# An encoder layer with two kinds of attention: when TensorE multiplies the attention weights with the values

## The chip, the cores and the metric

The kernel runs on one core of one Trainium2 chip. A core has five engines that run side by side and wait for each other through semaphores: TensorE (PE in the profile; its weight loads are shown apart as PEld), VectorE (DVE), ScalarE (ACT), GpSimd (POOL) and SyncE (SP), whose queue issues nearly all transfers here. Each engine works through its own instructions in the program's order. The metric is the device time of one execution in microseconds, and less is better. A time is given as the median of several runs.

## The reference, cut to what matters

The reference is one inference step of an encoder layer. Two streams are computed: a prompt of 2048 frames (new) and 8 running streams with 16 frames each and a cache of 512. What the change touches is the prompt's attention, which exists in two kinds. Per head and per tile of 128 queries:

```python
# branch a: differential attention, 4 heads, block-causal
s = einsum('bqhcd,bkhcd->bhcqk', q, k) * HEAD_DIM_A ** -0.5
p = softmax(where(mask, s, -inf))
w = p[:, :, 0] - lam * p[:, :, 1]
o = einsum('bhqk,bkhe->bqhe', w, v)
# branch b: stick-breaking attention, 8 heads, causal
z = einsum('bqhd,bkhd->bhqk', q, k) * HEAD_DIM_B ** -0.5
log_1m = where(mask, log_sigmoid(-z), 0)
log_a = log_sigmoid(z) + reverse_cumsum(log_1m) - log_1m
a = where(mask, exp(log_a), 0)
o = einsum('bhqk,bkhd->bqhd', a, v)
```

Around it stand a modulated norm, one wide input projection (queries, keys, values and gates of both branches), and behind it the merge of the branches, an output projection and a last norm.

## The kernel before, in words

All matrix products are made in float16 pairs: a number is split into a high and a low half, and two or three products are added up. The program has three stages. The first (to about 150 us of the profile) makes the modulation and the normed input. The second, the main loop (to about 1845 us), makes the projections and the prompt's attention. The third makes the merge, the output and the attention of the running streams.

**The main loop** runs over 8 units of 17 steps each. Even units are heads of the softmax kind (`kind` 0), odd units are pairs of heads of the stick kind (`kind` 1). In a unit the step `NT` (16) stands for the running streams' tile and has no attention in this loop; the steps 0 to 15 are the prompt's tiles of 128 queries. Tile t meets t + 1 blocks of 128 keys, so a step's work grows with t.

**One tile's attention** takes this way. TensorE multiplies queries with keys in chunks of up to 512 keys (`chunk`, L656, L657, and the mask with L660) into one of three score banks `ps_s`. VectorE (softmax kind, L575) or ScalarE and VectorE (stick kind, L123 and the scan L633) empty the bank into `sc_p` and `sc_n`. The weights follow: `softmax_pair` for the softmax kind, `stick_weights` (a product on POOL, L639) for the stick kind. `turn` splits them into halves (`sc_n` again) and lets SP issue a transposing transfer into a tile `wt` (L597). These tiles are a ring of 5 (`WT_BUFS`), and one holds a segment of up to 8 key blocks (`SEG`); a softmax tile has one segment up to t = 7 and two from t = 8, a stick tile twice as many, for its two heads. At last TensorE multiplies the transposed weights with the values, block by block (`pv_block`): three products of 128 columns for the softmax kind (L713 to L715), one of 128 and one of 64 for the stick kind (L717, L718), added up in one of two banks `ps_o`. `natural` and `store` then take the result out.

**What sets the order.** The program is written step by step, and in a step three streams are laid into each other by `interleave`: `pieces` of the projections of later tiles (two products of 512 columns each, L445 and L521), the score chunks `qk` of this step's tile, and the products with values `vs` of the tile two steps earlier (`PV_LAG = 2`). Each piece has a weight, and a stream's pieces are spread evenly over the step by their weights; the products with values are spread over the stretch from 0.1 to 1.0 of it. A scheduler then orders each engine's instructions once, when the program is built: it may draw an instruction ahead of another that it takes to be not ready yet. In the running program that order is fixed, so a product with values whose `wt` has not landed holds all that stands behind it on TensorE.

SP's queue is shared by the transposing transfers, the loads of projected inputs (`hs`, L422), the stores of results (`out_dram`, `o_d`, `z_d`, `g_d`) and the caches' loads.

Of the kernel before, what the change touches and what calls it, by code (L numbers as in the profile page):

```python
# [32 lines left out]
NT = SEQ // P  # L33
# [3 lines left out]
NEG = -3.0e38  # L37
STICK = 14
SEG = 8
PV_LAG = 2  # L40
WT_BUFS = 5
SC_BUFS = 6
V_LO, V_HI = 0.1, 1.0
W_READY = 9
WIDE_BUFS = 6
P0_AT = 2.0, 4.0, 6.0
# [45 lines left out]
    return c  # L92


def interleave(*streams):

    order = []
    for i, pieces in enumerate(streams):  # L100
        lo, hi = 0.0, 1.0
        if isinstance(pieces, tuple):
            pieces, lo, hi = pieces
        total = sum(cost for cost, _ in pieces) or 1.0
        done = 0.0
        for j, (cost, fn) in enumerate(pieces):
            order.append((lo + (hi - lo) * (done + cost / 2) / total, i, j, fn))
            done += cost
    for _, _, _, fn in sorted(order, key=lambda e: e[:3]):
        fn()  # L110


# [1 line left out]
def layer_kernel(ctx: ExitStack, tc: tile.TileContext, a: dict):  # L114
# [81 lines left out]
    def bank(tag, dt=F32):  # L196
        return ps.tile([P, 512 if dt == F32 else 1024], dt, tag=tag, name=f"ps_{tag}", bufs=BANKS[tag])
# [384 lines left out]
    def turn(job, seg, scale=None):  # L582

        nb = seg["hi"] - seg["lo"]
        nk = nb * P
        w16 = seg["n"].bitcast(F16)
        hi, lo, src = w16[:, 0:nk], w16[:, nk : 2 * nk], seg["p"][:, 0:nk]
        if scale is None:
            S.copy(out=hi, in_=src)  # L589
            V.tensor_tensor(out=lo, in0=src, in1=hi, op=ALU.subtract)  # L590
        else:
            split(hi, lo, src, scale, S)
        if job["t"] == NT:
            seg["wt"] = job["pool"].tile([P, 10, P], F16, tag="dwt", name="dwt", bufs=2)
        else:
            seg["wt"] = wtp.tile([P, 2 * SEG, P], F16, tag="wt", name="wt", bufs=WT_BUFS)
        nc.sync.dma_start_transpose(out=seg["wt"][:, 0 : 2 * nb, :], in_=w16[:, 0 : 2 * nk])  # L597

    def softmax_pair(job):

# [102 lines left out]
    def store(U, t, o):  # L703
        ui = (U["h"] + 4 * U["kind"]) * P
        if U["kind"] == 0:
            sum_squares(o, P, osums[:, t, U["h"] : U["h"] + 1])
        load(out=o_d[t][:, ui : ui + P], in_=o)
# [9 lines left out]
            T.matmul(po[:, c * P : (c + 1) * P], wt[:, wj, :], vt[:, c, :, :], start=first, stop=False)  # L717
            T.matmul(po[:, c * P : c * P + 64], wt[:, nb + wj, :], vt[:, c, 0, :], start=False, stop=last)  # L718

    def pv(job):  # L720

        U, t, c = job["U"], job["t"], job["c"]
        segs = job["segs"] if U["kind"] == 0 else job["segs"][::-1]
        order = [(seg, j) for seg in segs for j in range(seg["hi"] - seg["lo"])]

        def block(i):
            seg, j = order[i]
            if i == 0 and (U["kind"] == 0 or c == 0):
                U["po", t] = bank("o")
            pv_block(job, seg, U["po", t], j, U["v"][seg["lo"] + j], i == 0, i == len(order) - 1)  # L730
            if i == len(order) - 1 and (U["kind"] == 0 or c == 1):
                store(U, t, natural(U, t, U.pop(("po", t))))

        return [(1.5, lambda i=i: block(i)) for i in range(len(order))]

    def cache_column(name, h):
        return "ab".index(name[0]) * 4 + h
# [167 lines left out]
    steps = [(u, t) for u in range(8) for t in [NT] + list(range(NT))]  # L905
    back = []
    spare, cached = norms()
    jobs = []


    line = []
# [58 lines left out]
    with tc.tile_pool(name="p0", bufs=1) as p0:  # L970
# [28 lines left out]
        first = wide_tile().rearrange("p k n -> p (k n)")  # L999
# [207 lines left out]
    cuts = None  # L1207
# [98 lines left out]

        return [branch_weight for _ in branch_weights] + [rest] + [lambda t=t: first(t) for t in tiles[0:2]]

    for n in range(len(steps) + PV_LAG):
        made, qk, vs = [], [], []  # L1310
        if n < len(steps):
            u, t = steps[n]
            past += duration(t)
            if t == (3 if u == 0 else NT) and u < 7:
                back += prepare_unit(u + 1)
            if u == 7 and not back and not spare and not cached and len(branch_weights) > 1:
                branch_weight()
            for fn in back[: -(-len(back) // max(1, (W_READY if u else W_READY + 2) - t % NT))]:
                back.pop(0)()
            for todo, here in ((spare, norm_at), (cached, keys_at)):  # L1320
                if todo and here(u, t):
                    left = sum(here(*step) for step in steps[n:])
                    for _ in todo[: -(-len(todo) // left)]:
                        todo.pop(0)()
            if t < NT:
                qk = scores(units[u], t, made)
        if n >= PV_LAG:
            for job in jobs[n - PV_LAG]:
                vs += pv(job)
        target = position(len(steps) * past / whole + LEAD)  # L1330
        pieces = take(target, min(n + 1, len(steps) - 1))
        if at[0] == len(line) and not pieces and not spare and not cached:
            if cuts is None:
                cuts = early_work()
            pieces = [(1.0, fn) for fn in cuts[: -(-len(cuts) // (len(steps) + PV_LAG - n))]]
            del cuts[: len(pieces)]
        interleave(pieces, qk, (vs, V_LO, V_HI))
        jobs.append(made)
    c01.close()


    with ExitStack() as c2:
# [7 lines left out]
        vs = scales(total(add_up_all(csums), 8), res, "s_c", 8)  # L1350
# [147 lines left out]
```

## Time and profile before

| | |
|---|---|
| median of 3 runs | 2331.89 us (2329.62 to 2332.84) |
| the profiled execution's own time | 2323.62 us |
| its span, first to last instruction | 2321.8 us |
| VectorE busy | 1732.0 us (75%) |
| ScalarE busy | 1624.0 us (70%) |
| GpSimd busy | 689.0 us (30%) |
| DMA engines, share of the span, queue of SP | 76.3% |

The profile is one execution; its own time lies some 8 us under the median of the timed runs, so what is worked out from it is added to or taken from its own time first. Busy time of TensorE is modelled: products are pipelined, and one of 512 columns is shown with about 380 ns though the next one starts 215 ns later. The idle time ahead of an instruction, and what ended it, is the better measure of a wait. A granted clock (PEclk) of 0.50 means that TensorE's products run at half their speed.

### The profile page before, as it was taken

The numbers are of one execution on the slowest core, as the hardware profiler recorded it, in microseconds if no ns is written. First come the engines' busy times: TensorE is split into PE (matmuls) and PEld (weight loads), VectorE is DVE, ScalarE is ACT, GpSimd is POOL, SyncE is SP. The second block draws the span as 40 slices with busy tenths as digits, with TensorE's granted clock in tenths as the row PEclk, the third lists the DMA queues.
The fourth block names the chain that finished last, engine by engine and source line by source line (L and its number), as shares of the span: only waits on it lengthen the run. The fifth ranks groups of instructions, "written<-read, shape, count | busy, mean of one in ns | idle before, by whom it ended". The sixth has DMA issues, their size and how long they took to land. (4 is left out here: it accounts for less than half of the span.)

```text
span 2321.8 us, 41788 instructions
## 1 busy us (share of the span) xinstructions
PE 2100.0 (90%) x14752; PEld 1129.4 (49%) x14752; DVE 1732.0 (75%) x3795; ACT 1624.0 (70%) x3228; POOL 689.0 (30%) x610
## 2 busy tenths in 40 slices
PE   5998898998999989889998998999998689899998
PEld 3654454454555545455554454555454344444443
DVE  4648768779876777888767779687778878677663
ACT  3958677777876677978676887866678666566541
POOL 1223014346320334553024356310334312111211
PEclk8999999999999999999999999999999799999999
DMA  9777558888796788988878798566577899789431
GB/s 328 270 222 206 133 139 218 191 189 191 186 254 136 203 208 179 207 189 212 201 186 219 175 222 210 151 160 148 140 155 171 174 270 265 208 227 235 141 105 48
DMA packets 805827, 445.30 MB, mean 192 GB/s; under 512 B 537354, under 2 KB 744506, under 8 KB 805104
## 3 DMA queue, kind: packets, MB, share of 16 engines
q1 hardware_dynamic: 804668, 442.24, 76.3%
q8 instruction: 115, 1.88, 0.3%
q14 instruction: 96, 0.79, 0.1%
q10 hardware_dynamic: 948, 0.39, 0.1%
HBM read 228.82 MB, written 86.02 MB: 136 GB/s over the span
## 5 line engine op out<-in xcount | busy, mean ns | idle before, releaser
L639 POOL TENSOR_TENSOR sc_p<-sc_p,sc_n 128x127 f32<-128x127 f32 (+7 forms) x192 | 314.2, 1640 | 700.4 <-DVE sc_n L633 597.2
L445 PE MATMUL ps_mm<-wb,hs 128*128 128x512 f16 x1734 | 445.0, 383 | 2.0 <-DMA hs<-hT_d 2.0
L445 PEld LDWEIGHTS <-hs 128*128 128x128 f16 x3120 | 276.3, 99 | 252.9 <-issue 8.6
L445 PE MATMUL ps_mm<-wa,hs 128*128 128x512 f16 x1386 | 352.0, 383 | 2.0 <-DVE v L304 2.0
L633 DVE TENSOR_TENSOR_SCAN sc_n<-ps_s,sc_n,zero_t 128x512 f32<-128x512 f32 x192 | 245.5, 1279 | 70.5 <-ACT ps_s L123 65.2
L656 PE MATMUL ps_s<-k,qst 128*128 128x512 f16 (+3 forms) x640 | 226.8, 355 | 53.4 <-DVE sc_n L633 44.5
L521 PEld LDWEIGHTS <-hs 128*128 128x128 f16 x1632 | 155.4, 99 | 183.2 <-ACT qst L549 6.1
L590 DVE TENSOR_TENSOR sc_n<-sc_p,sc_n 128x128 f16<-128x128 f32 (+7 forms) x192 | 215.0, 1125 | 39.4 <-ACT sc_n L589 38.4
L123 ACT ACTIVATE sc_p<-ps_s,usc 128x512 f32<-128x512 f32 (+3 forms) x320 | 203.5, 636 | 37.0 <-PE ps_s L657 27.6
L657 PE MATMUL ps_s<-k,qst 128*128 128x512 f16 (+3 forms) x640 | 226.6, 355 | 0.0
L521 PE MATMUL ps_t<-wb,hs 128*128 128x512 f16 x918 | 219.5, 381 | 0.3 <-DVE qst L549 0.3
L717 PE MATMUL ps_o<-v,wt 128*128 128x128 f16 x1088 | 176.2, 228 | 45.1 <-DMA wt<-sc_n 44.8
L589 ACT CAST sc_n<-sc_p 128x128 f16<-128x128 f32 (+7 forms) x192 | 153.8, 806 | 70.4 <-POOL sc_p L639 67.4
L123 ACT ACTIVATE ps_s<-ps_s,usc 128x512 f32<-128x512 f32 (+3 forms) x328 | 198.8, 606 | 0.0
L1412 PE MATMUL ps_o<-wo,wa 128*128 128x512 f16 x816 | 183.0, 380 | 0.7 <-ACT wa L1224 0.7
L521 PE MATMUL ps_t<-wa,hs 128*128 128x512 f16 x714 | 173.0, 385 | 7.8 <-ACT qst L549 6.0
L717 PEld LDWEIGHTS <-wt 128*128 128x128 f16 x1088 | 107.5, 103 | 111.1 <-DMA wt<-sc_n 56.3
L718 PE MATMUL ps_o<-v,wt 128*128 128x64 f16 x1088 | 160.6, 200 | 0.0
L575 DVE TENSOR_SCALAR_CACHE_REDUCE sc_n<-ps_s,usc 128x512 f32<-128x512 f32 (+3 forms) x160 | 106.2, 664 | 37.9 <-PE ps_s L660 19.7
L718 PEld LDWEIGHTS <-wt 128*128 128x128 f16 x1088 | 105.0, 102 | 55.9 <-issue 2.5
L633 DVE TENSOR_TENSOR_SCAN sc_n<-ps_s,zero_t 128x128 f32<-128x128 f32 (+3 forms) x128 | 104.3, 815 | 34.5 <-ACT ps_s L123 33.6
L575 DVE TENSOR_SCALAR_CACHE_REDUCE sc_p<-ps_s,usc 128x512 f32<-128x512 f32 (+3 forms) x160 | 106.2, 664 | 30.9 <-PE ps_s L657 22.8
(369 smaller groups left out, 4438.7 us busy)
## 6 DMA issues: line engine op xcount, KB each, us to landing
hs<-hT_d SPq DMA_DIRECT2D x130, 512.0 KB, 4.4
g_d<-gt SPq DMA_DIRECT2D x68, 256.0 KB, 4.9
wb<-g_d SPq DMA_DIRECT2D x34, 512.0 KB, 4.3
out_dram<-pr SPq DMA_DIRECT2D x204, 64.0 KB, 2.6
wa<-in_w_in_dram SPq DMA_DIRECT2D x34, 256.0 KB, 5.7
o_d<-o SPq DMA_DIRECT2D x136, 64.0 KB, 2.4
hs<-o_d SPq DMA_DIRECT2D x17, 512.0 KB, 3.8
out_dram<-x SPq DMA_DIRECT2D x17, 512.0 KB, 2.8
```

The costliest lines, as they stand in the source:

```text
L123: i = S.activation(**kw)
L445: T.matmul(box["p"], box["h"][:, hi, k, :], U["w"][k][:, wi, :], start=(n == 0), stop=(n == 3 * KT - 1))
L521: T.matmul(box["g"][:, 0:gw], box["h"][:, hi, k, :], U["wg"][k // per][:, k % per, wi, :], start=(j == 0), stop=(j == 3 * KT - 1))
L575: V.tensor_scalar(out=dst[:, lo : lo + n], in0=p[:, 0:n], scalar1=sc_pos, scalar2=None, op0=ALU.mult, op1=ALU.max, accum_out=job["mx"][:, ...
L590: V.tensor_tensor(out=lo, in0=src, in1=hi, op=ALU.subtract)
L633: V.tensor_tensor_scan(out=dst[:, lo : lo + n][:, ::-1], data0=src[:, 0:n][:, ::-1], data1=zero_t[:, 0:1].to_broadcast([P, n]), initial=fi ...
L639: G.tensor_tensor(out=p[:, 0:m], in0=p[:, 0:m], in1=n[:, 1 : m + 1], op=ALU.mult)
L656: T.matmul(p[:, 0:n], qst[:, c, :], kk[:, c, 0:n], start=True, stop=False)
L657: T.matmul(p[:, 0:n], qst[:, 2 + c, :], kk[:, c, 0:n], start=False, stop=not diag)
L717: T.matmul(po[:, c * P : (c + 1) * P], wt[:, wj, :], vt[:, c, :, :], start=first, stop=False)
L718: T.matmul(po[:, c * P : c * P + 64], wt[:, nb + wj, :], vt[:, c, 0, :], start=False, stop=last)
L1412: T.matmul(po, st["y"][:, yi * 8 + k, :], wo[j * 4 + k // 2][:, wi, k % 2, :], start=(n == 0), stop=(n == 3 * KT - 1))
```

## The change

The products with values are no longer a stream of a step. `turn`, which issues a segment's transposing transfer, now appends that segment's products to a list `due`, with the mark `spent + 30`. `spent` counts the work given to TensorE, in estimated microseconds: 0.44 for a projection piece, 0.22 times its weight for a score chunk, 0.17 (softmax) or 0.085 (stick) for one block's products. `give` writes out the step's projection pieces and score chunks, still laid into each other evenly, and after each of them all products whose mark has been reached. The number of products, of transfers and of all other instructions is the same on every engine; only places change. What is left in `due` in the last step is written out as pieces of that step.

```diff
-PV_LAG = 2
+PV_LAG = 30.0
+PIECE, CHUNK, PV_A, PV_B = 0.44, 0.22, 0.17, 0.085
...
-V_LO, V_HI = 0.1, 1.0
...
-def interleave(*streams):
+def interleaved(*streams):
     order = []
     for i, pieces in enumerate(streams):
-        lo, hi = 0.0, 1.0
-        if isinstance(pieces, tuple):
-            pieces, lo, hi = pieces
         total = sum(cost for cost, _ in pieces) or 1.0
         done = 0.0
         for j, (cost, fn) in enumerate(pieces):
-            order.append((lo + (hi - lo) * (done + cost / 2) / total, i, j, fn))
+            order.append(((done + cost / 2) / total, i, j, cost, fn))
             done += cost
-    for _, _, _, fn in sorted(order, key=lambda e: e[:3]):
+    return [(i, cost, fn) for _, i, _, cost, fn in sorted(order, key=lambda e: e[:3])]
+
+
+def interleave(*streams):
+    for _, _, fn in interleaved(*streams):
         fn()
...
         nc.sync.dma_start_transpose(out=seg["wt"][:, 0 : 2 * nb, :], in_=w16[:, 0 : 2 * nk])
+        if job["t"] < NT:
+            cost = (PV_A, PV_B)[job["U"]["kind"]]
+            due.extend((spent[0] + PV_LAG, cost, fn) for fn in pv(job, seg))
...
-    def pv(job):
-
-        U, t, c = job["U"], job["t"], job["c"]
-        segs = job["segs"] if U["kind"] == 0 else job["segs"][::-1]
-        order = [(seg, j) for seg in segs for j in range(seg["hi"] - seg["lo"])]
-
-        def block(i):
-            seg, j = order[i]
-            if i == 0 and (U["kind"] == 0 or c == 0):
+    due, spent = [], [0.0]
+
+    def pv(job, seg):
+
+        U, t, c, i = job["U"], job["t"], job["c"], job["segs"].index(seg)
+        last_seg = len(job["segs"]) - 1 if U["kind"] == 0 else 0
+        first_seg = 0 if U["kind"] == 0 else len(job["segs"]) - 1
+        nb = seg["hi"] - seg["lo"]
+
+        def block(j):
+            first, last = i == first_seg and j == 0, i == last_seg and j == nb - 1
+            if first and (U["kind"] == 0 or c == 0):
                 U["po", t] = bank("o")
-            pv_block(job, seg, U["po", t], j, U["v"][seg["lo"] + j], i == 0, i == len(order) - 1)
-            if i == len(order) - 1 and (U["kind"] == 0 or c == 1):
+            pv_block(job, seg, U["po", t], j, U["v"][seg["lo"] + j], first, last)
+            if last and (U["kind"] == 0 or c == 1):
                 store(U, t, natural(U, t, U.pop(("po", t))))
 
-        return [(1.5, lambda i=i: block(i)) for i in range(len(order))]
+        return [lambda j=j: block(j) for j in range(nb)]
+
+    def give(order, costs):
+
+        for i, weight, fn in order:
+            fn()
+            spent[0] += weight * costs[i]
+            while due and due[0][0] <= spent[0]:
+                _, cost, product = due.pop(0)
+                product()
+                spent[0] += cost
...
-    for n in range(len(steps) + PV_LAG):
-        made, qk, vs = [], [], []
+    for n in range(len(steps) + 2):
+        made, qk = [], []
...
-        if n >= PV_LAG:
-            for job in jobs[n - PV_LAG]:
-                vs += pv(job)
...
-            pieces = [(1.0, fn) for fn in cuts[: -(-len(cuts) // (len(steps) + PV_LAG - n))]]
+            pieces = [(1.0, fn) for fn in cuts[: -(-len(cuts) // (len(steps) + 2 - n))]]
             del cuts[: len(pieces)]
-        interleave(pieces, qk, (vs, V_LO, V_HI))
-        jobs.append(made)
+            if n == len(steps) + 1:
+                pieces += [(PV_B / PIECE, fn) for _, _, fn in due]
+                due.clear()
+        give(interleaved(pieces, qk), (PIECE, CHUNK))
```

Two places of the built order show the move. The line numbers of the changed program are up to 15 higher (L597 is L598 there, L707 is L711, L717 and L718 are L721 and L722, L445 is L446).

The first place is SP's queue where the second stick unit begins. `wt<-sc_n` is a transposing transfer, and 128x2x128 is tile 0's (two for its two heads), 128x4x128 tile 1's and so on; `o_d_62<-o` stores the result of tile 0 of this unit, so it stands behind that tile's products, and `o_d_77` is the unit before's last tile. Before:

```order
L597 DMA_TRANSPOSE wt<-sc_n 128x2x128 x2
L331 DMA wa_171<-in_w_in_dram 128x4x128 x2
L707 DMA o_d_77<-o 128x128
L422 DMA hs_182<-hT_d_58 128x2048
L889 DMA keys_ak_133<-wb_1429 128x2048
L869 DMA wa_176<-in_cache_a_k_dram 128x8x128
L597 DMA_TRANSPOSE wt<-sc_n 128x4x128
L525 DMA g_d_100<-gt_1421 128x512
L707 DMA o_d_62<-o 128x128
```

With the change, at the same place of the unit:

```order
L598 DMA_TRANSPOSE wt<-sc_n 128x6x128
L711 DMA o_d_77<-o 128x128
L598 DMA_TRANSPOSE wt<-sc_n 128x6x128
L906 DMA keys_ak_136<-wb_1433 128x2048
L886 DMA wb_1426<-in_cache_b_k_dram 128x8x128
L598 DMA_TRANSPOSE wt<-sc_n 128x8x128 x2
L502 DMA out_dram<-pr 128x128
L503 DMA out_dram<-pr 128x128
L711 DMA o_d_62<-o 128x128
```

Tile 0's store stood behind one transfer of tile 1; now it stands behind both of the tiles 1, 2 and 3.

The second place is TensorE in the later half of the same unit, where a tile has two segments of weights. Before, one block's two products stand between projection products:

```order
L445 LDWEIGHTS hs_180
L445 MATMUL ps_mm<-wb_1430,hs_180 128x512
L717 LDWEIGHTS wt
L717 MATMUL ps_o<-v,wt 128x128
L718 LDWEIGHTS wt
L718 MATMUL ps_o<-v,wt 128x64
L445 LDWEIGHTS hs_180
L445 MATMUL ps_mm<-wb_1431,hs_180 128x512
```

With the change a segment's blocks follow each other; these are the last of them, and what comes behind:

```order
L721 LDWEIGHTS wt
L721 MATMUL ps_o<-v,wt 128x128
L722 LDWEIGHTS wt
L722 MATMUL ps_o<-v,wt 128x64
L446 LDWEIGHTS hs_180
L446 MATMUL ps_mm<-wa_172,hs_180 128x512
```

The products of a segment moved together into one run, ahead of which and behind which the projections and scores follow without products between them.

More of the change, by code (lines that the diff above doesn't have):

```diff
@@ L907, in layer_kernel @@
     spare, cached = norms()
-    jobs = []
     line = []
```

## The prediction

> **What bounds the kernel now.** I read the page first, then the stretches, then TensorE's waits.
>
> ```profile
> span 2321.8 us, 41788 instructions
> PE 2100.0 (90%) x14752; PEld 1129.4 (49%) x14752; DVE 1732.0 (75%) x3795; ACT 1624.0 (70%) x3228; POOL 689.0 (30%) x610
> ```
>
> TensorE is the busiest engine, so its idle time is what can be won. The next view gives, by stretch (main loop, the loop's end, third stage): length, busy time of PE, PEld, DVE, ACT and POOL, PEclk, DMA share, GB/s.
>
> ```profile
> 150.00:1764.00 1614.00, 1490.52 (x10398) 807.22 (x10397) 1257.35 (x2678) 1214.46 (x2597) 539.68 (x477) 0.98 0.78 185
> 1764.00:1845.00 81.00, 54.97 (x468) 34.57 (x467) 70.72 (x97) 58.53 (x98) 40.40 (x25) 0.79 0.81 176
> 1845.00:2322.00 477.00, 432.23 (x3055) 209.96 (x3053) 326.09 (x758) 258.96 (x354) 79.81 (x60) 0.97 0.70 188
> ```
>
> TensorE is idle for 1614 - 1490.5 = 123.5 us of the loop and for 81 - 55 = 26 us of its end. The third stage has no part in the change. TensorE's waits over loop and end (total, times, longest):
>
> ```profile
> PE ps_o L717 <- DMA wt<-sc_n: 44.8, 28, 4.3
> PE ps_s L656 <- DVE sc_n L633: 44.5, 47, 2.5
> PE ps_o L713 <- DMA wt<-sc_n: 22.0, 16, 2.8
> ```
>
> Products with values wait 44.8 + 22.0 = 66.8 us for transposed weights: 2.9% of the span, and the change can touch no other wait directly. One such wait, in order of time:
>
> ```profile
> 1203.47 0.22 PE L660 MATMUL ps_s<-masks,idb 128*128 128x128 bf16 x1
> ...
> 1214.22 3.62 SPq L597 DMA_TRANSPOSE wt<-sc_n  x2
> ...
> 1214.28 0.22 PE L717 MATMUL ps_o<-v,wt 128*128 128x128 f16 x1
> ...
> 1214.33 0.19 PE L718 MATMUL ps_o<-v,wt 128*128 128x64 f16 x1
> ...
> 1214.36 0.22 PE L717 MATMUL ps_o<-v,wt 128*128 128x128 f16 x1
> ...
> 1217.31 0.23 PE L717 MATMUL ps_o<-v,wt 128*128 128x128 f16 x1 [2.52 <-DMA wt<-sc_n]
> ```
>
> The last mask product of tile 3's scores starts at 1203.5; its transfer is issued at 1214.2, and the product at 1217.3 has waited 2.5 us. So the way from scores to usable weights takes 13.8 us here, while the program holds only about 11 us of other work between.
>
> **Where these waits lie.** The first four rows are the tiles 0 to 7 of the four stick units, the last is the end of the loop.
>
> ```profile
> PE ps_o L717 <- DMA wt<-sc_n: 3.7, 3, 2.8
> PE ps_o L717 <- DMA wt<-sc_n: 5.3, 3, 2.5
> PE ps_o L717 <- DMA wt<-sc_n: 4.9, 4, 2.5
> PE ps_o L717 <- DMA wt<-sc_n: 1.2, 2, 0.8
> PE ps_o L717 <- DMA wt<-sc_n: 16.6, 10, 4.3
> ```
>
> Short stick tiles: 3.7 + 5.3 + 4.9 + 1.2 = 15.1. The loop's end: 16.6. The rest of L717, 44.8 - 15.1 - 16.6 = 13.1, falls on the last tiles of the long stick steps. The softmax units have the 22.0 of L713.
>
> **How far the change moves the products.** For each of the 288 transfers I counted, in both orders, TensorE's work from the last score product to the first product with values, with prices from these rows:
>
> ```profile
> 1197.74 1.46 PE L445 MATMUL ps_mm<-wb,hs 128*128 128x512 f16 x6
> ```
>
> Six of 512 columns take (1.46 - 0.38)/5 = 0.216 us each; above, a product of 128 columns takes 1214.33 - 1214.28 = 0.05 and one of 64 takes 0.03. Medians, before and now: short stick tiles (64 transfers) 14.2 and 27.0 us; the last three tiles of the stick units 1, 3 and 5 (36) 18.7 and 21.1; softmax units (96) 19.0 and 22.0; the loop's end (16) 5.7 and 5.5. It isn't 30 everywhere, because the build holds scores back behind projections while the products keep their place.
>
> **The terms of the sum.**
>
> Short stick tiles: the distance grows by 13 us and the longest wait is 2.8. All 15.1 go. Bounds 0 (the transfers get later by as much, a rival below) and -15.1. I take -15.
>
> Softmax units: 16 waits of 1.4 us on average stand against 3 us more distance in the median, but single transfers gain nothing or come 4 us nearer. Bounds 0 and -22; I take -10.
>
> Last stick tiles: 13.1 against 2.4 us more. Bounds 0 and -13; I take -5.
>
> The loop's end: nothing is left there to put ahead of the products, and the distance shrinks by 0.2. Bounds +6 (ten waits, each up to 0.6 longer) and -3; I take 0.
>
> The clock. After some of these waits TensorE ran at half speed:
>
> ```profile
> 1101.44 0.23 PE L713 MATMUL ps_o<-v,wt 128*128 128x128 f16 x1 [1.98 <-DMA wt<-sc_n]
> ```
> ```profile
> 218.70:222.10 3.40, 3.40 (x30) 2.85 (x28) 0.66 (x3) 1.55 (x4) 0.00 (x0) 0.51 0.62 157
> ...
> 1102.70:1106.10 3.40, 3.40 (x23) 2.39 (x21) 2.38 (x11) 2.60 (x5) 0.00 (x0) 0.50 0.98 266
> 1413.30:1420.10 6.80, 4.85 (x23) 2.47 (x24) 6.80 (x7) 3.62 (x6) 4.17 (x5) 0.50 1.04 240
> sum 27.20, PE 24.35 PEld 15.11 DVE 19.63 ACT 17.43 POOL 9.06; mean PE 4.06 PEld 2.52 DVE 3.27 ACT 2.90 POOL 1.51
> ```
>
> Six stretches, 27.2 us in all, stand at 0.50 right behind waits for `wt` ahead of the loop's end, which costs 13.6 us of TensorE's time. With 30 of 50 us of the waits gone I take about half back, -6; bounds 0 and -13. [...]
>
> The runs. 351 more products stand directly behind another product (counted: 3063 before, 3414 now). In the rows above such products start 0.05 and 0.03 us apart, so a run costs nothing more: 0. [...]
>
> Score banks. The 44.5 us of L656 come where TensorE asks for a bank before VectorE's scan has emptied it. Between a chunk and the third behind it the lowest tenth of the distances is 4.9, 5.0 and 4.6 us in the units 1, 3 and 5 before, and 4.7, 5.4 and 5.7 now: 0, bounds -10 and +25.
>
> Sum: -15 - 10 - 5 + 0 - 6 + 0 + 0 = **-36**, of which I hold back 5, since TensorE, once ahead, meets some wait of another kind sooner: -31. On the profiled execution that is 2323.6 - 31 = 2292.6; on the median of the runs, 8.3 higher, 2331.9 - 31 = **2301**. Its own range takes each term part of the way to its bounds: -15, -16, -9, -1, -8 and 0 make -49, and -10, -4, -2, +3, -2 and +3 make -12 (tiles, softmax, last tiles, end, clock, banks): 2283 to 2320.
>
> **The rivals.**
>
> *The ring of five.* A `wt` tile is now held longer, so the transfer of the fifth segment behind it stands at the head of SP's queue until the products are through, and the loads of `hs` behind it come late. For it:
>
> ```profile
> SPq L597 <- PE ps_o L718: 57.0, 31, 4.2
> ```
>
> SP already loses 57.0 us in 31 waits for products, and in SP's order above six later transfers stand ahead of tile 0's store, where it was one. Against it: by the same count the freeing product ended up to 18.7 us after the new segment's last scores, and now up to 15.6; 18 transfers are over 13 us in both. It decides where a load passed to TensorE late. If 18 transfers hold the queue for another 4.2 us, that is 76 us, and if half of it reaches TensorE and half of the gain is lost: 2331.9 + 38 - 15 = 2355. Chance 0.17.
>
> *The wait moves.* The 31 us come back at the score banks, since in the stick units VectorE is the next engine:
>
> ```profile
> 770.00:995.00 225.00, 201.94 (x1407) 107.27 (x1406) 179.95 (x278) 174.82 (x350) 100.25 (x81) 0.97 0.84 196
> ```
>
> It is busy for 180 of 225 us, 80%; that leaves room, and the distances above don't shrink. About 2328. Chance 0.15.
>
> *It doesn't do what it says.* The build reorders, and sets products early again as it did before; in the softmax units it nearly does. If only the short tiles' 15 are won and 15 lost elsewhere: 2332. Chance 0.03.
>
> *More.* All waits ahead of the loop's end, their clock and some of the banks' go: 50 + 13 + 10 = 73, so 2259; half way, 2270. Chance 0.11.
>
> **How the numbers follow.** My forecast has 0.54. The range of 8 in 10 reaches from 2266 (most of "more") to 2345 (the wait moves, and the milder half of the ring). Within 0.2% (4.7 us), about what a measurement of this kernel can tell from no change: 0.10, from "the wait moves" (0.07) and "it doesn't" (0.03). Faster: 0.54 + 0.11 + 0.05 of "the wait moves" = 0.70. Slower: 0.17 + 0.03 = 0.20.
>
> **What would show it.** In the changed profile the L717 and L713 rows should hold about 35 us of waits for `wt` together, half of it in the loop's last 80 us, and next to none in the tiles 0 to 7 of the stick units. L656 should stay near 44, PEclk of the loop come to 0.99, and L445 still wait next to nothing for `hs`. If waits for `hs` or at SP for L718 rise by tens of us, the ring was the cause; if L656 rises by 25, the wait moved. I am wrong in size if the softmax units keep all of their 22.

## The result, and the profile after

The changed kernel takes 2303.51 us (median of 6 runs, 2296.17 to 2309.85). The kernel before, run beside it, takes 2327.9 us (6 runs; the three ahead of the prediction were at the upper end of these). The ratio is 0.9896 with a 95% interval of 0.9868 to 0.9924: the change saves 24 us, or between 18 and 31. The prediction was 2301 us, by a gain of 31.

The profiled execution of the changed kernel took 2304.59 us, 19.0 less than that of the kernel before. Its page begins:

```profile
span 2302.8 us, 41756 instructions
PE 2098.3 (91%) x14752; PEld 1130.4 (49%) x14752; DVE 1724.1 (75%) x3795; ACT 1622.1 (70%) x3228; POOL 697.6 (30%) x610
```

The work is the same: the 32 instructions that are fewer in all are semaphore instructions, every other kind has the same count. The main loop and its end (columns as in the prediction) show where the time went:

```profile
150.00:1743.00 1593.00, 1489.88 (x10423) 810.91 (x10422) 1250.17 (x2678) 1206.28 (x2586) 542.59 (x474) 0.99 0.81 188
1743.00:1825.00 82.00, 51.91 (x434) 31.27 (x433) 67.29 (x92) 57.02 (x96) 41.85 (x25) 0.77 0.77 162
```

Ahead of the loop's end TensorE is idle for 1593 - 1489.9 = 103 us where it was 123.5, and its granted clock there is 0.99 where it was 0.98. At the loop's end it is idle for 30 us where it was 26. TensorE's waits over the loop and its end (total, times, longest):

```profile
PE ps_s L660 <- DVE sc_n L637: 45.7, 49, 2.8
PE ps_o L721 <- DMA wt<-sc_n: 25.2, 16, 6.9
PE ps_o L717 <- DMA wt<-sc_n: 14.7, 10, 3.8
PE ps_s L660 <- DVE sc_n L576: 9.1, 7, 3.3
PE ps_t L522 <- DVE qst L550: 6.5, 5, 3.0
PE ps_t L221 <- DVE qst L550: 6.0, 2, 3.5
PE ps_s L660 <- DVE sc_p L576: 4.7, 9, 1.3
PE ps_s L221 <- ACT junk L282: 4.2, 2, 2.6
```

The waits for `wt` went from 66.8 to 39.9 us. The scan's row stays near its 44.5. The banks that VectorE's step of the softmax units empties (L575, now L576) had these rows before:

```profile
PE ps_s L656 <- DVE sc_p L575: 3.9, 5, 2.0
PE ps_s L656 <- DVE sc_n L575: 2.4, 5, 1.0
```

Now they have 4.7 and 9.1 us, and two rows on L221 (small products that sum over the partitions), which were not there before, hold 10 us. The waits of L721 for `wt` in the stick units ahead of the loop's end stand in three rows, since one unit has none, and the last row is the loop's end:

```profile
PE ps_o L721 <- DMA wt<-sc_n: 4.0, 4, 1.3
...
PE ps_o L721 <- DMA wt<-sc_n: 2.3, 1, 2.3
...
PE ps_o L721 <- DMA wt<-sc_n: 0.8, 1, 0.8
...
PE ps_o L721 <- DMA wt<-sc_n: 18.0, 10, 6.9
```

The 7.1 us of the first three hold the tiles 0 to 7 and the last tiles. Sorted by transfer, 2.7 us fall on the tiles 0 to 7 (15.2 before), 4.5 on the last tiles (12.9), 14.9 on the softmax units (22.0) and 18.0 on the loop's end (16.6).

The tile whose late transfer the prediction showed reads like this now (timeline of TensorE and SP; tile 3 of the third stick unit):

```profile
1183.37 0.31 PE L664 MATMUL ps_s<-masks,idb 128*128 128x128 bf16 x1
...
1199.76 4.44 SPq L598 DMA_TRANSPOSE wt<-sc_n  x2
...
1211.97 0.22 PE L721 MATMUL ps_o<-v,wt 128*128 128x128 f16 x1
```

The transfer is even later behind the scores than before, 16.4 us where it was 10.7. But the product comes 28.6 us behind them and waits for nothing. This is the change's effect in one place: the transfer didn't get faster, other work fills the time.

**Where the loop's time went.** The next table sums up the trace from 150 us to the end of the last product with values, for the two kernels: TensorE's idle time by what ended it (gaps over 0.1 us), and half of the time at a granted clock of 0.50, which is about what the lower clock costs (products of 128 columns start 0.10 to 0.11 us apart at 0.50 and 0.05 to 0.07 at full clock). The remainder is what is left, mostly work at full clock.

| us | before | after |
|---|---|---|
| length | 1690.4 | 1672.5 |
| waits for `wt` | 66.8 | 40.1 |
| waits for `hs` | 2.0 | 0 |
| waits for the score banks' readers (`sc_n`, `sc_p`) | 54.3 | 61.8 |
| all other waits | 25.1 | 30.5 |
| half of the time at clock 0.50 | 47.8 | 42.7 |
| remainder | 1494.4 | 1497.4 |

Of the 26.7 + 2.0 + 5.1 us won, 7.5 + 5.4 + 3.0 are given back, and 17.9 are left. The rest of the span's 19.0 lies behind the loop.

### The profile page after: what moved, and what is told of

The parts are those of the page before. It is cut to its first block, busy times and chain, and to the rows that moved or that the text cites. A ratio compares the mean times of both kernels' runs of the same rounds, so it can differ in the third digit from the quotient of the medians.

```text
span 2302.8 us, 41756 instructions
## 1 busy us (share of the span) xinstructions
PE 2098.3 (91%) x14752; PEld 1130.4 (49%) x14752; DVE 1724.1 (75%) x3795; ACT 1622.1 (70%) x3228; POOL 697.6 (30%) x610
## 5 line engine op out<-in xcount | busy, mean ns | idle before, releaser
L643 POOL TENSOR_TENSOR sc_p<-sc_p,sc_n 128x127 f32<-128x127 f32 (+7 forms) x192 | 314.5, 1640 | 744.7 <-DVE sc_n L637 505.3
L446 PEld LDWEIGHTS <-hs 128*128 128x128 f16 x3120 | 293.7, 99 | 312.6 <-issue 7.9
L446 PE MATMUL ps_mm<-wb,hs 128*128 128x512 f16 x1734 | 433.8, 382 | 0.0
L446 PE MATMUL ps_mm<-wa,hs 128*128 128x512 f16 x1386 | 338.9, 380 | 1.9 <-DVE v L305 1.9
L660 PE MATMUL ps_s<-k,qst 128*128 128x512 f16 (+3 forms) x640 | 225.4, 353 | 61.5 <-DVE sc_n L637 45.7
L522 PEld LDWEIGHTS <-hs 128*128 128x128 f16 x1632 | 156.3, 99 | 188.5 <-DVE qst L550 12.2
L721 PE MATMUL ps_o<-v,wt 128*128 128x128 f16 x1088 | 132.4, 225 | 25.3 <-DMA wt<-sc_n 25.2
L576 DVE TENSOR_SCALAR_CACHE_REDUCE sc_p<-ps_s,usc 128x512 f32<-128x512 f32 (+3 forms) x160 | 106.2, 663 | 43.8 <-PE ps_s L661 28.4
L487 POOL TENSOR_TENSOR rot<-pr,rope 128x256 f32<-128x256 f32 x68 | 60.5, 889 | 245.9 <-ACT pr L460 202.8
L721 PEld LDWEIGHTS <-wt 128*128 128x128 f16 x1088 | 102.0, 102 | 55.0 <-DMA wt<-sc_n 31.8
L1427 PEld LDWEIGHTS <-wa 128*128 128x128 f16 x816 | 78.6, 98 | 95.3 <-issue 2.6
L722 PE MATMUL ps_o<-v,wt 128*128 128x64 f16 x1088 | 123.7, 197 | 0.0
```

Of the source, the lines that this page charges most:

```text
L446: T.matmul(box["p"], box["h"][:, hi, k, :], U["w"][k][:, wi, :], start=(n == 0), stop=(n == 3 * KT - 1))
L522: T.matmul(box["g"][:, 0:gw], box["h"][:, hi, k, :], U["wg"][k // per][:, k % per, wi, :], start=(j == 0), stop=(j == 3 * KT - 1))
L643: G.tensor_tensor(out=p[:, 0:m], in0=p[:, 0:m], in1=n[:, 1 : m + 1], op=ALU.mult)
L660: T.matmul(p[:, 0:n], qst[:, c, :], kk[:, c, 0:n], start=True, stop=False)
L1427: T.matmul(po, st["y"][:, yi * 8 + k, :], wo[j * 4 + k // 2][:, wi, k % 2, :], start=(n == 0), stop=(n == 3 * KT - 1))
```

## The experiments

Each kernel is an edit of the changed kernel. Its ratio is against the kernel before, run beside it. This table has the same columns for all of them; the last one is the number of loads of `hs` which by the built order have less than 6 us of TensorE's work between the last product that reads the buffer's old content and the first that needs the new (a load takes 4.1 to 5.0 us in the median to land).

| kernel | median us | ratio (95%) | loop | `wt` | `hs` | banks | other | clock | rem. | short loads |
|---|---|---|---|---|---|---|---|---|---|---|
| change | 2303.5 | 0.9896 (0.9868 to 0.9924) | 1672.5 | 40.1 | 0 | 61.8 | 30.5 | 42.7 | 1497 | 1 |
| lag16 | 2378.4 | 1.0224 (1.0204 to 1.0243) | 1735.5 | 89.3 | 37.7 | 34.8 | 16.6 | 61.4 | 1496 | 22 |
| short16 | 2321.3 | 0.9977 (0.9961 to 0.9993) | 1686.5 | 55.2 | 4.4 | 57.2 | 24.9 | 49.5 | 1495 | 2 |
| long16 | 2354.4 | 1.0081 (1.0056 to 1.0106) | 1716.1 | 60.7 | 10.1 | 66.7 | 18.0 | 71.2 | 1489 | 4 |
| lag38 | 2307.0 | 0.9911 (0.9893 to 0.9929) | 1671.0 | 28.0 | 0 | 76.2 | 35.4 | 38.7 | 1493 | 0 |
| soft38 | 2317.5 | 0.9926 (0.9904 to 0.9949) | 1676.6 | 34.1 | 0 | 68.2 | 31.1 | 54.3 | 1489 | 0 |
| spread | 2318.0 | 0.9946 (0.9926 to 0.9967) | 1676.6 | 34.3 | 16.6 | 54.8 | 32.6 | 41.9 | 1496 | 8 |
| wt4 | 2311.2 | 0.9930 (0.9911 to 0.9949) | 1673.2 | 39.0 | 5.9 | 70.6 | 12.8 | 52.9 | 1492 | 1 |
| s4 | 2355.7 | 1.0118 (1.0100 to 1.0136) | 1714.9 | 14.6 | 18.2 | 49.2 | 72.4 | 58.0 | 1502 | 23 |
| s4lag24 | 2357.3 | 1.0127 (1.0112 to 1.0142) | 1723.7 | 43.8 | 10.4 | 43.8 | 55.7 | 64.9 | 1505 | 7 |
| lag16hsg | 2442.2 | 1.0459 (1.0436 to 1.0482) | 1802.2 | 144.2 | 14.5 | 36.4 | 22.8 | 93.4 | 1491 | 14 |
| hsg | 2362.8 | 1.0121 (1.0097 to 1.0146) | 1718.1 | 63.6 | 0 | 53.8 | 44.5 | 52.9 | 1503 | 0 |
| lead6 | 2353.2 | 1.0076 (1.0048 to 1.0104) | 1717.9 | 41.6 | 0 | 71.2 | 40.0 | 58.0 | 1507 | 0 |

The columns count every gap over 0.1 us up to the loop's last product with values, so they can differ by a few tenths from the rows of a view. The remainder lies between 1489 and 1507 everywhere, so waits and clock account for the larger differences in the loop's length, and differences of some 10 us can lie in the remainder. Where it is 1502 or more, 28 to 95 more products of other work lie ahead of the loop's last product with values.

### lag16: the distance nearly halved

```diff
-PV_LAG = 30.0
+PV_LAG = 16.0
```

> The changed kernel with a distance of 16 in place of 30. Counted in its order, TensorE's work between the last scores and the first product with values has medians of 15 us (short stick tiles), 14 (long stick tiles), 15 (last stick tiles) and 20 (softmax), near or below the kernel before. Distance theory (the gain comes from the work put between a transfer and its products): waits for wt of 70 to 110 us where the change has 40 and the kernel before 67, and 2325 to 2360 us (ratio to before 1.00 to 1.015). Rival, the runs (the gain comes from products that stand in one run, and scores that are no longer broken up by them): the runs are the same, so the time stays within 0.3% of the change, ratio 0.990. Rival, the ring of five: a shorter hold frees the ring and SP's queue, faster than the change.

2378.38 us. TensorE's waits:

```profile
PE ps_o L721 <- DMA wt<-sc_n: 53.4, 42, 6.2
PE ps_mm L446 <- DMA hs<-hT_d: 37.6, 21, 3.9
PE ps_o L717 <- DMA wt<-sc_n: 35.5, 19, 4.1
PE ps_s L660 <- DVE sc_n L637: 21.4, 27, 1.7
```

The waits for `wt` more than double (by kind: softmax 35.7, short stick tiles 17.4, middle ones 9.0, last ones 10.0, loop's end 17.3). So the distance is what removed them. It isn't the runs of products: more of them stand directly behind another here (3501) than in the change (3414). The run is slower than the theory foretold, because projections wait for `hs`, which they do not in the change. I first put this down to SP's queue, where transfers stand ahead of the loads. Three later runs test it.

### short16: half the distance for the short stick tiles alone

```diff
+            lag = 16.0 if job["U"]["kind"] == 1 and job["t"] < 8 else PV_LAG
-            due.extend((spent[0] + PV_LAG, cost, fn) for fn in pv(job, seg))
+            due.extend((spent[0] + lag, cost, fn) for fn in pv(job, seg))
```

> The changed kernel with a distance of 16 for the stick kind's tiles 0 to 7 alone, 30 for all else; the median there falls from 27 to 17 us (14 in the kernel before). Distance theory: the waits for wt in those tiles come back from 2.7 to 8 to 13 us, all others stay, and the kernel is 6 to 14 us slower than the change, ratio 0.992 to 0.996. If the short tiles' waits were made up elsewhere, no difference to the change (0.990). Ring theory: the short tiles hold the ring less, faster than the change.

2321.28 us, 18 over the change. The waits for `wt`:

```profile
PE ps_o L722 <- DMA wt<-sc_n: 36.9, 28, 6.9
PE ps_o L718 <- DMA wt<-sc_n: 17.9, 11, 3.3
```

Those of the short tiles go from 2.7 to 16.0 us, which is the 15.2 of the kernel before again; the other kinds stay within 3.5. The loop grows by 14.0 (waits for `wt` +15.1, clock +6.8, `hs` +4.4; banks and others give 10.2 back, the remainder 2.0). That is more than the 6 to 14 us that the theory gave. Of the 24 us that the change saves 18 are gone with this edit, so the short stick tiles, with what moves along with them, carry about three quarters of its gain.

### lag38: more distance

```diff
-PV_LAG = 30.0
+PV_LAG = 38.0
```

> The changed kernel with a distance of 38 in place of 30; medians by its order 30.5, 35, 28 and 26.5 us. Distance theory: the softmax and last stick waits that are left (15 + 4.5 us) go nearly all, waits for wt 40 -> 20 to 25, nearly all of it in the loop's end; 2290 to 2297 us, ratio 0.983 to 0.987. Ring theory: the product that frees a wt buffer ends over 13 us after the new segment's scores for 69 transfers where it is 18 now, so SP's waits for the stick products grow from 29 us to over 60, transfers and hs loads land later, and the kernel is slower than the change, ratio 0.993 or more. Runs theory: as the change, 0.990.

2307.01 us, the same as the change within the intervals, where the distance theory gave 2290 to 2297. TensorE's waits:

```profile
PE ps_s L660 <- DVE sc_n L637: 57.9, 46, 5.8
PE ps_o L721 <- DMA wt<-sc_n: 23.2, 11, 5.3
...
PE ps_o L717 <- DMA wt<-sc_n: 4.7, 6, 1.8
```

The waits for `wt` fall to 28.0, of which 23.2 are the loop's end, which no distance reaches. So 12.1 us are won there, and 14.4 more are spent at the score banks. So beyond a distance of 30 the waits changed their place here, and no time was won.

### soft38: more distance for the softmax units alone

```diff
+            lag = 38.0 if job["U"]["kind"] == 0 else PV_LAG
-            due.extend((spent[0] + PV_LAG, cost, fn) for fn in pv(job, seg))
+            due.extend((spent[0] + lag, cost, fn) for fn in pv(job, seg))
```

> The change with a distance of 38 for the softmax units alone, 30 elsewhere. Theory (what is won at wt from here on is given back at the score banks): softmax waits for wt fall from 14.9 to about 5 us, the others stay (short 3, last 5, end 18), score-bank waits rise by 5 to 10 us, 2298 to 2310 us. Rival (lag38 lost its gain only through the stick units' ring): softmax waits fall by 10 and nothing rises, 2285 to 2296 us.

2317.45 us. The softmax units' waits for `wt` fall from 14.9 to 11.9 only, those of all kinds by 6.0, and the banks take 6.4. The clock costs 11.6 more, the remainder 8.5 less; the profiled loop is 4 us longer, and the third stage, which the edit doesn't touch, 8 us. The time is over what the theory gave, but the exchange of `wt` against banks is of the kind that it foretold, though small: only 3 us went of the 10 expected. The rival, that the stick units' ring alone cost lag38 its gain, finds no support: nothing is won here either.

### spread: no runs of products

With this edit `give` writes out at most one block's products after each piece.

```diff
-            while due and due[0][0] <= spent[0]:
+            if due and due[0][0] <= spent[0]:
```

> The changed kernel, but at most one block's products are written out behind each projection piece or score chunk, so that a segment's blocks no longer stand in one run; medians of the distance 28, 28, 23 and 24 us, as in the change or a little more. Distance theory: same waits for wt (35 to 45 us), ratio 0.987 to 0.993. Runs theory: most of the gain goes, ratio 0.996 or more.

2318.01 us, about 14 over the change; the ratio lies between what the two theories gave. The loss does not come from waits for `wt`, which are 34.3. TensorE's waits for loads:

```profile
PE ps_mm L446 <- DMA hs<-hT_d: 16.6, 8, 5.3
```

The built order has 8 short loads here and TensorE 8 such waits, so what `hs` costs comes with the order. The ring has little part in it: it held SP's transfers for 22.2 us in 21 cases, in the change for 18.2 us in 15 (how these are told apart stands behind the experiments, at the ring of five). In the profiled loop only 4 us of the loss are seen, and 6 us behind it, which the edit doesn't touch. A run of products does no harm that this shows; whether it is worth something stays open, since the order, and with it the loads, moved as well.

### wt4: a ring of four

```diff
-WT_BUFS = 5
+WT_BUFS = 4
```

> The changed kernel with a ring of four wt buffers in place of five; the distances by its order stay (22, 26, 26.5 and 22 us). Ring theory, as a rival to the account that the ring has room: SP's waits for the stick products rise from 29 us to over 80, the transfers land later, waits for wt or for hs on TensorE come back by 20 us or more, ratio 1.00 or more. If the ring of five has room to spare: within 0.4% of the change, ratio 0.987 to 0.994.

2311.19 us, 8 over the change, and the intervals of the two ratios overlap. The ring held SP's transfers for 29.5 us in 27 cases, where it was 18.2 us in 15. The waits for `wt` stay (39.0), those for `hs` become 5.9. So the ring limits little: one tile less costs some 8 us. A larger one was not tried.

### s4 and s4lag24: a fourth score bank

The fourth bank is taken from the products with values, which have one bank in place of two; the third stage's products alternate between the two sets.

```diff
-    BANKS = {"mm": 2, "s": 3, "t": 1, "o": 2}
+    BANKS = {"mm": 2, "s": 4, "t": 1, "o": 1}
...
-                po = bank("o")
+                po = bank("so"[j])
```

s4lag24 has `PV_LAG = 24.0` as well.

> The changed kernel with four score banks and one bank for the products with values (it had three and two; the third stage's output product takes its second bank from the scores). Distance as written stays 30, but the build no longer holds the scores back as far, so the medians by its order are 29 us (softmax), 29 and 27 (stick). Theory, the score banks now limit: with the waits for wt down, what is left of TensorE's idle time in the loop is the wait for a score bank (45.7 us for the scan, 9.1 and 4.7 for the softmax copies in the change). With a fourth bank these fall to 20 to 30 and the waits for wt ahead of the loop's end from 22 to under 8: 15 to 35 us off the loop, ratio to before 0.975 to 0.984. Rival, VectorE limits (80% busy in the stick units): the waits move to the transposing transfers or the single product bank, the loop stays as long as the change's, ratio 0.988 to 0.995.

> Four score banks and a distance of 24; medians by its order 25 us (softmax), 26, 23 and 22 (stick), about the change's. Distance theory: the same waits for wt as the change (35 to 42 us) with the fewer bank waits of the run above; 3 to 10 us slower than the run above. Ring theory (a longer hold in wt costs SP's queue time): faster than the run above, as only 7 transfers wait over 13 us for their buffer by the order in place of 25.

2355.68 and 2357.27 us, both slower than the kernel before, which neither the theory nor the rival gave for s4. TensorE's waits in s4:

```profile
PE ps_s L660 <- DVE sc_n L637: 30.2, 21, 3.6
PE ps_t L535 <- ACT gt L525: 21.2, 10, 5.5
PE ps_mm L446 <- DMA hs<-hT_d: 18.2, 18, 4.4
...
PE ps_o L721 <- DVE o L702: 7.9, 4, 4.5
```

The waits at the score banks and for `wt` fall as they should, to 49.2 and 14.6 us together 38 less than in the change. But 18 us more of waits for `hs`, 42 of others and 15 of clock come in their place, and products with values wait for their single bank to be emptied (L702). Scores also start 11 us later. So the edit does not show what score banks alone are worth, because the bank that it takes is needed and because the built order moves elsewhere.

### lag16hsg and hsg: the loads of `hs` on another queue

lag16hsg is lag16 with this edit, hsg the change with it.

```diff
-        load(out=ahead[u, t], in_=hT_d[t // 4][:, t % 4, :, :, :])
+        nc.gpsimd.dma_start(out=ahead[u, t], in_=hT_d[t // 4][:, t % 4, :, :, :])
```

> The distance of 16 again, as in lag16 (2378 us, 37.6 us of waits for hs, where the change has none), but with the loads of hs issued on GpSimd's queue, so that they no longer stand behind transposing transfers and stores on SP's. Theory (held transfers at SP's head make the loads late): TensorE's waits for hs fall under 12 us, those for wt stay near 90, the run takes 2330 to 2355 us. Rival (the loads are late because their buffers come free late): waits for hs stay over 25 us, the run stays over 2365. Third way: GpSimd's own queue holds the loads as long, and its weight products come late as well: hs over 25 and wt over 100 us.

> The change with nothing but the loads of hs moved to GpSimd's queue. The change has no waits for hs, so by the theory there is nothing to win from them: 2295 to 2315 us, waits for wt 35 to 45 us. What it could bring is a freer SP queue (29 us of waits for the ring's products stay), what it could cost is GpSimd's time: each load's issue stands between its weight products. If SP's queue still cost the change time that is not seen as a wait for hs, the run is under 2292.

2442.19 and 2362.81 us: 64 and 59 us slower than the same without the edit, and far from the 2295 to 2315 expected of hsg. GpSimd's waits in hsg:

```profile
POOL sc_p L643 <- DVE sc_n L637: 352.1, 141, 14.9
POOL hs L423 <- PE ps_t L522: 310.8, 33, 34.8
```

GpSimd now waits 310.8 us, up to 34.8 at a time, for TensorE to release the buffers, and its weight products L643 stand behind. That makes the weights late: waits for `wt` of 63.6 in hsg and 144.2 in lag16hsg. The waits for `hs` in lag16hsg fall to 14.5, neither under 12 nor over 25, so this pair does not decide between SP's queue and late buffers. Two things speak for the buffers. In lag16's trace 15 of the 22 loads that came late were issued within 2 us of the end of the last product that reads their buffer, 8 of these at once, so SP held only the others for longer. And GpSimd, with nothing of SP's ahead of the loads, waited for the buffers itself.

### long16: half the distance everywhere else

```diff
+            lag = PV_LAG if job["U"]["kind"] == 1 and job["t"] < 8 else 16.0
-            due.extend((spent[0] + PV_LAG, cost, fn) for fn in pv(job, seg))
+            due.extend((spent[0] + lag, cost, fn) for fn in pv(job, seg))
```

> A distance of 16 everywhere but at the stick units' tiles 0 to 7, which keep 30 (the median distance is 19.8 / 18.4 / 15.3 / 14.8 us by the built order for softmax / short / middle / last stick tiles, where lag16 had 19.7 / 15.2 / 14.3 / 14.8). By the built order only 4 of 127 loads of hs have less than 6 us of TensorE's work between the last product that reads the old content of their buffer and the first that needs the new, against 22 in lag16 and 1 in the change. Theory (the waits for hs of lag16 come from the built order, which lets the buffers go late, and not from what stands ahead of the loads on SP's queue): waits for hs 3 to 10 us against 37.6, waits for wt 65 to 90 us, 2330 to 2355 us. Rival (SP's queue holds the loads, since its transfers are waited for as in lag16): waits for hs stay over 20 us, over 2360 us.

2354.40 us, inside what the theory gave.

```profile
PE ps_mm L446 <- DMA hs<-hT_d: 10.1, 7, 2.2
```

The waits for `hs` go from 37.6 to 10.1 us (21 to 7 of them). SP's queue is held by its transfers as much as in lag16, where the largest row of this kind has 102.5 us in 52 waits:

```profile
SPq L598 <- DVE sc_n L591: 102.6, 45, 6.5
```

Over all kernels here the number of these waits follows the last column of the table (22 short loads and 21 waits, 23 and 18, 14 and 8, 8 and 8, 7 and 7, 4 and 7, 2 and 2, 1 and none to 3, none and none). So the loads come late mainly because the order that the build makes lets a buffer go too shortly before its next use, and my reading by SP's queue falls as the main cause. The waits for `wt` sum to 60.7, a little under the theory's 65 to 90. Most of the 44 us that the loop loses to the change is clock (+28.5) and `wt` (+20.6).

### lead6: the projections one step earlier

```diff
-LEAD = 5.0
+LEAD = 6.0
```

> The change with the projections set one step earlier (6 in place of 5). By the built order the distances are 23.4 / 27.6 / 28.4 / 17.3 us (softmax / short / middle / last stick tiles; the change has 22.0 / 27.0 / 27.8 / 21.1), no load of hs has less than 6 us, and the ring holds fewer segments long. Distance theory: softmax waits for wt fall by 2 to 5 us, the last tiles' rise by 2 to 6, the sum stays near 40; 2295 to 2312 us, the same as the change within what can be told. Rival (the distance decides little, the waits are handed on anyway by where the projections stand): over 2315 or under 2290 us with the sum of the waits for wt still near 40.

2353.19 us. The waits for `wt` sum to 41.6, as in the change, and the time is 50 us longer: the rival came true. TensorE's waits:

```profile
PE ps_s L660 <- DVE sc_n L637: 52.6, 54, 3.1
PE ps_o L721 <- DMA wt<-sc_n: 23.1, 14, 7.5
PE ps_o L717 <- DMA wt<-sc_n: 18.2, 14, 3.3
PE ps_s L660 <- DVE sc_n L576: 10.9, 9, 3.0
```

By kind the waits for `wt` did not go as the distances: in the softmax units the distance grew and the waits rose from 14.9 to 18.2. In the profiled loop's 45 us, 9.4 are score banks, 9.5 other waits, 1.5 `wt`, 15.3 clock, and 9.7 lie in the remainder (66 more products of other work ahead of the loop's end). So the waits for `wt` alone do not set the time; a built order that is as good for them can be worse for the rest. How waits turn into time at half clock stands in the last section; why this order's waits fall worse stays open.

None of these versions beats the change.

## Why the prediction was right, and where it was not

**The mechanism** held. More of TensorE's work between a transfer and its products removes waits for `wt`, and short16 and lag16 bring them back.

**The terms**, foretold and measured in the profiled execution:

| term | foretold | measured |
|---|---|---|
| short stick tiles | -15 | -12.5 (15.2 to 2.7) |
| softmax units | -10 | -7.1 (22.0 to 14.9) |
| last stick tiles | -5 | -8.4 (12.9 to 4.5) |
| the loop's end | 0 | +1.4 (16.6 to 18.0) |
| the clock | -6 | -5.1 (95.6 to 85.3 us at half speed) |
| runs | 0 | at most +3.0 (the remainder) |
| score banks | 0 | +7.5 |
| held back for other waits | +5 | +3.4 (others +5.4, `hs` -2.0) |
| sum | -31 | -17.9 in the loop, -19.0 in all |

The waits themselves came to -26.6 where -30 was foretold: right in size and in place, since each kind is near its term.

The step that was mis-sized is "Score banks": I took 0, within bounds of -10 and +25, because the built order's distances between the chunks don't shrink. That count was of the stick units 1, 3 and 5, and there it held: the scan's row has 45.7 us where it had 44.5. What grew are the banks of the softmax units, which the count left out (6.3 to 13.8 us). The distance is also counted in TensorE's work, not in time. As I read it, when TensorE waits less between two chunks, the same work takes less time, while VectorE's step takes as long as ever (a scan of 512 columns 1.28 us in the median, before and now); so part of each wait removed ahead of a bank comes back at the bank. The exchange shows most plainly in lag38, there in the scan's row (57.9): 12.1 us won at `wt`, 14.4 lost at the banks. It isn't shown bank by bank, since s4 moved too much else, and not every run has it: in long16 the waits for `wt` rise by 20.6 us and those for banks by 4.9 as well. The rival "the wait moves" was right in kind, and in size it was a quarter of what it foretold.

**The clock.** The loop ahead of its end did run at 0.99, and the time at half speed there fell from 61.4 to 47.8 us. The term was worked out from the stretches behind waits for `wt`. These fell from 27.3 to 10.2 us, which is worth 8.5; stretches behind other waits (34.1 to 37.5) and in the loop's end (34.2 to 37.5) gave 3.4 of it back. One such place in the changed kernel, in the timeline and in the stretches right before and behind it:

```profile
206.10 0.23 PE L717 MATMUL ps_o<-v,wt 128*128 128x128 f16 x1 [2.27 <-DMA wt<-sc_n]
206.17 0.22 PE L718 MATMUL ps_o<-v,wt 128*128 128x128 f16 x1
206.22 0.26 PE L719 MATMUL ps_o<-v,wt 128*128 128x128 f16 x1
206.28 0.31 PE L717 MATMUL ps_o<-v,wt 128*128 128x128 f16 x1
206.38 0.31 PE L718 MATMUL ps_o<-v,wt 128*128 128x128 f16 x1
```

```profile
205.00:206.30 1.30, 0.20 (x4) 0.20 (x5) 1.30 (x3) 1.21 (x2) 0.64 (x1) 0.99 1.11 207
206.30:209.70 3.40, 3.40 (x27) 2.67 (x25) 3.11 (x11) 1.18 (x3) 0.00 (x0) 0.50 1.04 321
```

A wait of 2.27 us ended in a stretch of 3.40 us at 0.50, and the products' starts went from 0.05 to 0.10 us apart. The measured -5.1 is near the -6 taken from such stretches of the kernel before.

**The runs** cost nothing that shows: spread, which breaks them up, is not faster, and in the rows above, at full clock, products of 128 columns start 0.05 to 0.07 us apart. The remainder, in which a cost of theirs would lie, rose by 3.0.

**The ring of five** was the rival with the highest price, and it did not come. The row that the prediction took for it fell from 57.0 us in 31 waits:

```profile
SPq L598 <- PE ps_o L722: 29.2, 20, 4.5
```

But this row is no measure of the ring. The built order tells whose tile each transfer takes over. Where the ring holds one, the trace shows it start 0.22 us (in a few cases up to 0.34) behind the start of the last product that reads the old content, with SP waiting ahead of it. One such place in the changed kernel, on SP and on TensorE:

```profile
882.81 0.32 SPq L526 DMA_DIRECT2D g_d<-gt  x1
886.62 1.76 SPq L598 DMA_TRANSPOSE wt<-sc_n  x1
```

```profile
886.40 0.19 PE L722 MATMUL ps_o<-v,wt 128*128 128x64 f16 x1
```

Counted so, the ring held SP for 16.7 us in 12 transfers before and for 18.2 us in 15 now, and only 3 of the row's 31 waits are among the 12. So the rival's 57.0 us were over three times too many, and the change neither adds to the ring's waits nor takes any away. That fits the reason against the rival, that by the built order a tile comes free no later behind the new scores. In lag38 it is 12.5 us in 15, and no wait for `hs`. The rival's price, 38 us, was far too high: a ring of four, with 29.5 us of such waits, costs some 8 us.

**"More"**, that all waits ahead of the loop's end go with their time, falls: lag38 removes all but 4.8 us of them and is no faster.

**The number.** In the profiled executions the gain is 19.0, so the forecast was 12 us too large there. In the timed runs it is 24, since the kernel before came out at 2327.9 in more runs and the change below its profiled execution. So 2301 lies 2.5 us from the median, and that nearness is in part luck. The observations foretold held: half of the waits for `wt` in the loop's end, the row of the scan's bank near 44 (45.7), the clock at 0.99, no wait for `hs`. What I had not named is that the softmax units' banks and L221 would take part of the gain back.

**The loop's end** still waits, as expected, because nothing is left there. The last two segments:

```profile
1802.65 0.19 PE L722 MATMUL ps_o<-v,wt 128*128 128x64 f16 x1
1806.42 0.29 PE L721 MATMUL ps_o<-v,wt 128*128 128x128 f16 x1 [3.58 <-DMA wt<-sc_n]
...
1807.62 0.26 PE L722 MATMUL ps_o<-v,wt 128*128 128x64 f16 x1
1814.76 0.29 PE L721 MATMUL ps_o<-v,wt 128*128 128x128 f16 x1 [6.88 <-DMA wt<-sc_n]
```

A segment's products last 1.2 us, and the next transfer comes 7 us later.

## What to carry to other kernels

Where an engine waits for a transfer, a distance counted in its own work can remove the wait (here 66.8 us of them became 39.9), and where it was short and other work is left to fill it, it paid most here. Reckon with part of the gain coming back (here 15.9 of 33.8 us) at the next resources in line, here above all the banks that another engine empties; a still longer distance (lag38) won nothing more. In a program whose order is built by a scheduler every such number also moves other things, so compare all waits and the clock, not only the wait that was aimed at.

## What the runs showed of the hardware that was not expected

Idle time cost more than itself in these runs. Between the change and long16 the idle time of the loop differs by 23 us (132.4 and 155.5) and the time at half clock by 57 us (85.3 and 142.3), which costs another 28; between short16 and the change these are 9 and 14 us. The share differs from order to order, so the cost of the clock can't be read from the sum of the waits.

The traces show where the clock fell. In all 14 profiled loops it changed only at marks that lie whole multiples of 3.41 us apart, and the change went with TensorE's idle time (gaps over 0.1 us) between the last two marks. Of the stretches of 3.41 us at full clock, none of the 6069 with under 1.5 us of idle time was followed by half clock, all of the 202 with over 2.1 us were, and of the 251 between them 86 (in the kernel before and the change alone: none of 874, all of 23, and 10 of 34). Half clock went on behind all of the 158 stretches at half clock that had over 0.8 us, and ended behind 230 of the 231 with under 0.4 us (in these two: all of 19, and all of 30). From these counts I estimate that a wait of some 2 us that lies between two marks can cost about another 1.7 us (half of 3.41), and the same wait cut in two by a mark nothing more.

In hsg the loads of `hs` on GpSimd's queue (the tile's view; least, median and longest duration in ns):

```profile
L423 POOL DMA_DIRECT2D hs<-hT_d x130: 527/591/727, 106.9 to 1761.7; - x130
```

Issuing one takes 0.59 us, but one whose buffer was not free yet held GpSimd up to 34.8 us, and what stood behind it came late. So the queue of an engine that computes was a poor place here for loads that may have to wait: hsg took 59 us more than the change.
